# Mixture of experts in rounds of 3, 2, 2 and 1 with 64-row token tiles, wider weight rows, and six raw with three split weight buffers

## The chip, the core and the metric

The kernel runs on one core of a Trainium2 chip. The metric is device time in microseconds (us), the median of repeated executions. One execution is also profiled; its trace gives each engine's instructions, the transfers and the waits. The engines are TensorE (PE in the rows, PEld for its loads of stationary operands), VectorE (DVE), ScalarE (ACT), GpSimd (POOL) and SyncE (SP), whose queue issues the weight transfers.

## The reference, cut to what matters

A model of four blocks works on 256 tokens of 1024 features in float32. The part that the change touches is the mixture of experts at the end of the second block:

```python
def moe_ffn(x, router_w, w1, w3, w2):
    logits = (xt @ router_w).astype(F32)
    top_v, top_i = lax.top_k(logits, TOP_K)            # TOP_K = 2 of 8
    ...
    for e in range(N_EXPERTS):
        y = y + gates[:, e:e + 1].astype(x.dtype) * swiglu(xt, w1[e], w3[e], w2[e])
```

`swiglu(x, w1, w3, w2)` is `(silu(x @ w1) * (x @ w3)) @ w2`, with `w1` and `w3` of 1024 x 3584 and `w2` of 3584 x 1024 for each expert, 44 MB an expert. The inputs are fixed. The reference's router puts 134, 122, 80, 51, 48, 37, 28 and 12 tokens on its eight experts, in order of size; every other stage of the model works on all 256 tokens.

## The kernel before, in words

**Units.** All weights come as units of up to 1 MiB: `unit` (L168) has SyncE load 128 x 2048 floats into a raw buffer (tag `raw`), and `split` (L164) makes two float32r parts of it, `wh` on ScalarE (L165) and the rest `wl` on VectorE (L166). TensorE multiplies with both. Raw buffers come from pool `pw`, pairs `wh`/`wl` from pool `ph` (four of each before). SyncE may load a unit when VectorE has read the raw buffer's last content; the split may write when TensorE is done with the pair's last content.

**Slots.** `route` (L801) sorts the experts by their tokens: slot 0 has the most. The counts choose one of two plans, `few` or `many`, by a branch on a register. The inputs take `few`:

```python
few = [([(0, 0, False), (0, self.cap, True), (7, 0, True), (6, 0, True)],
        [[(0, (0, 1), None), (7, (2,), 0), (6, (3,), 1)]])]
few += [([(1, 0, False)], [one(1)])]
few += [([(s, 0, False), (s + 1, 0, False)], [one(s), one(s + 1, 1)]) for s in (2, 4)]
```

So the first round works on three experts in turn: slot 0 with a full tile of 128 tokens and a half tile of 64, and slots 7 and 6 with a half tile each. Slots 1 to 5 then have a full tile each, one expert after the other.

**Phases.** The hidden 3584 columns are cut in seven pieces `f` of 512. For one expert and one `f`, `up` (L952) takes two units each of `w1` and `w3` (four k-tiles of 128 rows, 512 columns), `turn` (L986) transposes the product (`uT`), and `down` (L1005) takes two units of `w2` (two k-tiles, 1024 columns): six units in all. A full tile needs three products for each k-tile and 512 columns (`wh` and `wl` with the high part of the tokens, `wh` with the low part), a half tile two, since its high and low parts lie side by side in one stationary operand of 128 columns and `wl` meets only the 64 high ones. In the trace a full tile shows as `ul`, a half tile as `uhl`. `phases` (L1149) alternates the experts of a round and puts `down` of a phase behind `up` of the next one. `finish` weighs the outputs and puts them back on their tokens. Slots 7 and 6 add their outputs up in SBUF (`ysum`), all other tiles in PSUM banks.

**Order.** `stream` (L1063) emits a unit's load and split two units ahead of the products. Each engine works through a list of its own that the compiler puts in order from this; engines wait on semaphores. The pools' sizes are one input of that order, so lists outside the mixture of experts change a little as well.

Of the kernel before, what the change touches and what calls it, by code (L numbers as in the profile page):

```python
# [11 lines left out]
F32R = mybir.dt.float32r  # L12
# [63 lines left out]
class Acc:  # L76
    """a PSUM region that n matmuls accumulate in; fresh: the first one clears the bank"""
# [30 lines left out]
class Gated:  # L108
    """a generator that comes to a halt ahead of job n until ready()"""
# [16 lines left out]
def blend(a, b, every):  # L126
    """a, with a step of b emitted after each `every` us of it"""
# [10 lines left out]
class Model:  # L138
# [145 lines left out]
    def run_a(self, src, c0, n, parts, x, nk=8, layout=None):  # L284
        """feature-layout product; parts: (bank, rows, column offset in bank, column offset in the unit)"""
# [19 lines left out]
    def feat(self, src, c0, nf, x, out):  # L305
        """nf tiles of 128 features, two to a bank: [128, f%2, tok]"""
# [3 lines left out]
    def to_feat(self, src, t, xh, xl):  # L310
        """src [128 tok, 1024] -> xh/xl[:, k, t*128:...] split transposed"""
# [20 lines left out]
    def bcast_row(self, dst, src):  # L332
        """DRAM vector [n] to all partitions of dst [128, n]"""
# [3 lines left out]
    def warm(self, func, after):  # L337
        """has the scalar engine's table for func loaded ahead of its use, once after [128, n] is there"""
# [6 lines left out]
    def rsqrt(self, v, eps):  # L345
        """v = (v + eps) ** -0.5 for a few columns, without a table of the scalar engine"""
# [1544 lines left out]
```

## Time and profile before

| | |
|---|---|
| median of 3 runs | 2378.1 us (2375.16 to 2379.86) |
| profiled execution, first to last instruction | 2376.3 us |
| mean granted TensorE clock | 0.989 of 2.4 GHz |
| first round of experts | about 447 to 855 us |
| rounds of slots 1 to 5 | about 855 to 1472 us |
| TensorE, VectorE, ScalarE busy | 96%, 74%, 59% of the span |

Busy times are sums over the span, so an engine with 74% can still be the limit of one stage. The stages are told apart by the windows in the section on rows. The trace gives no other time of the profiled execution than its span.

### The profile page before, as it was taken

How to read it: one execution, taken by the hardware profiler on the slowest of the kernel's cores; microseconds unless marked ns; L12 is line 12 of the kernel's file. 1: busy time of each engine (PE TensorE's matmuls, PEld its weight loads, DVE VectorE, ACT ScalarE, POOL GpSimd, SP SyncE). 2: the span in 40 equal slices, each digit the busy share in tenths (PEclk: the TensorE clock that was granted, in tenths of full speed). 3: DMA queues.
4: the chain of work that ended last, by engine and by line, in shares of the span. 5: the costliest groups of instructions: out<-in, count | busy, mean ns of one | idle time of the engine just before them, and what ended most of it. 6: DMA issues, size and time to landing. Idle time of an engine off the chain costs nothing. (4 is left out here: it accounts for less than half of the span.)

```text
span 2376.3 us, 29764 instructions
## 1 busy us (share of the span) xinstructions
PE 2285.2 (96%) x11444; PEld 1854.5 (78%) x11444; DVE 1770.3 (74%) x1907; ACT 1410.7 (59%) x1532; POOL 109.3 (5%) x154
## 2 busy tenths in 40 slices
PE   7999999799999989999999998899999999999998
PEld 6788886577777768887888776787888888888887
DVE  4665465798888998889888887898566459966653
ACT  5554354577777767677777775547554344764542
POOL 2100010100000000000000000100100001010000
PEclk9999999899999999999999999899999999999999
DMA  9456560699999989999999998553655554555552
GB/s 289 171 194 181 177 206 22 230 337 342 343 341 315 322 317 350 348 361 353 375 336 368 358 347 302 190 179 116 213 183 182 195 184 131 183 168 199 181 187 75
DMA packets 266967, 585.10 MB, mean 246 GB/s; under 512 B 10513, under 2 KB 21189, under 8 KB 266560
## 3 DMA queue, kind: packets, MB, share of 16 engines
q1 hardware_dynamic: 260880, 565.48, 68.7%
q0 software_dynamic: 5936, 17.64, 2.4%
q8 instruction: 91, 1.49, 0.3%
q14 instruction: 60, 0.49, 0.1%
HBM read 580.43 MB, written 2.64 MB: 245 GB/s over the span
## 5 line engine op out<-in xcount | busy, mean ns | idle before, releaser
L166 DVE TENSOR_TENSOR wl<-raw,wh 128x2048 fp32r<-128x2048 f32 (+2 forms) x532 | 1200.9, 2269 | 391.6 <-ACT wh L165 389.4
L165 ACT ACTIVATE wh<-raw 128x2048 fp32r<-128x2048 f32 (+2 forms) x532 | 1003.5, 1895 | 515.4 <-PE lin L84 145.1
L945 PE MATMUL lin<-wh,ring 128*128 128x512 f32 x1680 | 556.1, 392 | 0.0
L945 PE MATMUL lin<-wl,ring 128*128 128x512 f32 (+1 forms) x1008 | 399.0, 396 | 9.4 <-DVE wl L166 9.3
L945 PEld LDWEIGHTS lin<-wh,ring 128*128 128x128 f32 x1680 | 315.4, 188 | 81.2
L945 PEld LDWEIGHTS lin<-wl,ring 128*128 128x128 f32 (+1 forms) x1008 | 171.3, 170 | 63.2 <-DVE wl L166 23.2
L84 PE MATMUL lin<-wh,hh 128*128 128x512 f32 x352 | 142.0, 404 | 0.0
L84 PE MATMUL lin<-wl,hh 128*128 128x512 f32 x352 | 138.4, 393 | 2.3 <-DVE wl L166 2.3
L84 PE MATMUL lin<-wh,hl 128*128 128x512 f32 x352 | 138.0, 393 | 0.1
L945 PE MATMUL y<-wl,uh 128*128 128x512 f32 x336 | 107.6, 401 | 3.8 <-DVE wl L166 3.8
L1427 DVE SCALAR_TENSOR_TENSOR ro<-conv,ro 128x256 f32<-128x256 f32 x240 | 105.5, 474 | 0.4
L945 PE MATMUL y<-wh,ul 128*128 128x512 f32 x336 | 104.3, 391 | 0.0
L945 PE MATMUL y<-wh,uh 128*128 128x512 f32 x336 | 104.1, 390 | 0.0
L84 PE MATMUL lin<-wh,h2h 128*128 128x512 f32 x256 | 101.1, 395 | 0.0
L84 PE MATMUL lin<-wl,h2h 128*128 128x512 f32 x256 | 99.9, 390 | 0.2
L84 PE MATMUL lin<-wh,h2l 128*128 128x512 f32 x256 | 99.3, 390 | 0.2
L84 PE MATMUL lin<-wh,xah 128*128 128x512 f32 (+1 forms) x240 | 87.7, 366 | 0.7 <-ACT xah L165 0.6
L84 PE MATMUL lin<-wh,xal 128*128 128x512 f32 (+1 forms) x240 | 86.7, 364 | 0.0
L84 PE MATMUL lin<-wl,xah 128*128 128x512 f32 (+1 forms) x240 | 86.6, 361 | 0.0
L84 PEld LDWEIGHTS lin<-wl,hh 128*128 128x128 f32 x352 | 66.8, 190 | 16.1 <-DVE wl L166 3.2
L84 PEld LDWEIGHTS lin<-wh,hh 128*128 128x128 f32 x352 | 66.8, 190 | 15.7 <-issue 1.3
L84 PEld LDWEIGHTS lin<-wh,hl 128*128 128x128 f32 x352 | 66.7, 189 | 14.7 <-DVE hl L166 0.4
(543 smaller groups left out, 3781.0 us busy)
## 6 DMA issues: line engine op xcount, KB each, us to landing
raw<-in_moe_w SPq DMA_DIRECT2D x336, 1024.0 KB, 6.8
raw<-in_w_in SPq DMA_DIRECT2D x70, 1024.0 KB, 5.2
raw<-in_w_ff SPq DMA_DIRECT2D x64, 1024.0 KB, 5.2
raw<-in_ffn_w SPq DMA_DIRECT2D x32, 1024.0 KB, 5.1
raw<-in_w_out SPq DMA_DIRECT2D x12, 1024.0 KB, 8.2
raw<-in_w_branch SPq DMA_DIRECT2D x8, 1024.0 KB, 5.9
raw<-in_w_out SPq DMA_DIRECT2D x8, 512.0 KB, 8.3
raw<-in_w_branch SPq DMA_DIRECT2D x8, 512.0 KB, 6.4
```

The costliest lines, as they stand in the source:

```text
L84: nc.tensor.matmul(o, lhsT=lhsT, rhs=rhs, start=(self.i == 0 and self.fresh), stop=(self.i == self.n - 1), skip_group_check=True)
L165: self.nc.scalar.activation(h, src, AF.Copy)
L166: self.nc.vector.tensor_sub(l, src, h.bitcast(F32))
L945: nc.tensor.matmul(a.ap[:rows], lhsT=lhsT, rhs=u[part][:, kk, cs], start=(a.i == 0), stop=(a.i == a.n - 1), skip_group_check=True)
L1427: nc.vector.scalar_tensor_tensor(acc[:, f], uT[:, f, k:k + 256], cw[:, f, k:k + 1], acc[:, f], op0=OP.mult, op1=OP.add)
```

## The change

- `route` also tells whether slot 3 has at most 64 tokens; a third plan, `light`, is run then. It keeps the first round, and pairs slot 1 (full tile) with slot 5 (half tile), slot 2 with slot 4, and takes slot 3 (half tile) alone. With the reference's counts slot 3 has 51 tokens.
- An expert has a new argument `wide`, true where each expert of a round has one tile: all rounds but the first. `up` and `down` then take two `f` at a time, and a unit of `w1` or `w3` is two k-tiles by 1024 columns. In the first round the order is by pairs of `f` too: each expert does two pieces before the next one's turn.
- `w2` has a new layout `pairs` in all rounds: a partition holds two neighbouring rows, 8 KB in one piece; `turn` takes every second column of the product to match.
- The pools have six raw buffers and three split pairs in place of four and four.
- The first write of `ysum` goes from VectorE to ScalarE. Comments are taken out.

```diff
-        self.pw = ctx.enter_context(tc.tile_pool(name="pw", bufs=4))
-        self.ph = ctx.enter_context(tc.tile_pool(name="ph", bufs=4))
+        self.pw = ctx.enter_context(tc.tile_pool(name="pw", bufs=6))
+        self.ph = ctx.enter_context(tc.tile_pool(name="ph", bufs=3))
...
+        elif layout == "pairs":
+            nc.sync.dma_start(rv, src[ks[0] * 128:(ks[0] + nk) * 128, c0:c0 + n].rearrange("(p k) n -> p k n", k=nk))
...
+        nc.vector.tensor_scalar(fit[:, 3:4], cs[:, 3:4], 64.5, fit[:, 2:3], op0=OP.is_lt, op1=OP.mult)
+        nc.vector.tensor_add(fit[:, 4:5], fit[:, 2:3], fit[:, 3:4])
...
-        def up(f):
+        def up(f, nf):
             accs = {}
+            kn = 4 // nf
...
+                ks = list(range(kn * q, kn * q + kn))
...
-                            accs[name, i] = Acc(self.bank("lin"), 8 * per[i])
-                        products(z, z["x"], ks, u, [(accs[name, i], slice(0, 512))])
-                return (wt, ks, f * 512, 512), work
+                            accs[name, i] = [Acc(self.bank("lin"), 8 * per[i]) for _ in range(nf)]
+                        products(z, z["x"], ks, u, [(accs[name, i][c], cols(c)) for c in range(nf)])
+                return (wt, ks, f * 512, 512 * nf), work
...
+                    part = lambda j: s[:, 256 * (j // 2) + j % 2:256 * (j // 2) + 256:2]
...
-                return (w2, [4 * f + 2 * q, 4 * f + 2 * q + 1], 0, 1024), work
+                k = 4 * (f + c) + 2 * q
+                return (w2, [k, k + 1], 0, 1024, "pairs"), work
...
+        steps = [[(f, 2)] if wide else [(f, 1), (f + 1, 1)] for f in (0, 2, 4)] + [[(6, 1)]]
...
-                for f in range(7):
+                for i in range(4):
                     for e in es:
-                        jobs = e[0](f)
...
+                        for p in e[5][i]:
+                            jobs = e[0](*p)
...
+        first = ([(0, 0, False), (0, self.cap, True), (7, 0, True), (6, 0, True)],
+                 [[(0, (0, 1), None), (7, (2,), 0), (6, (3,), 1)]])
+        light = [first]
+        light += [([(s, 0, False), (h, 0, True)], [[(s, (0,), None), (h, (1,), None)]]) for s, h in ((1, 5), (2, 4))]
+        light += [([(3, 0, True)], [one(3)])]
...
+        with tc.If(n > 1) as cmp:
+            run(light)
```

Two places show how the lists move. The first is VectorE's list in the first round, in the middle of it, ahead of a `ul`; `wl` is the split of a unit, `sa<-lin,sa` the first step of a half tile, `sa<-sa,lin` the product of the two branches, `ul` and `uhl` the split of a transposed full or half tile. Before:

```order
L166 TENSOR_TENSOR uhl<-uT,uhl 128x4x64
L166 TENSOR_TENSOR wl<-raw,wh 128x2048 x3
L971 TENSOR_TENSOR sa<-lin,sa 64x512
L166 TENSOR_TENSOR wl<-raw,wh 128x2048
L980 TENSOR_TENSOR sa<-sa,lin 128x512
L166 TENSOR_TENSOR wl<-raw,wh 128x2048
L980 TENSOR_TENSOR sa<-sa,lin 128x512
L166 TENSOR_TENSOR wl<-raw,wh 128x2048
L1024 TENSOR_TENSOR ysum<-ysum,y 128x512 x2
L166 TENSOR_TENSOR wl<-raw,wh 128x2048
L166 TENSOR_TENSOR ul<-uT,uh 128x512
```

And now, from the piece between two `ul` that lies in slots 7 and 6:

```order
L166 TENSOR_TENSOR uhl<-uT,uhl 128x4x64
L166 TENSOR_TENSOR wl<-raw,wh 128x2048
L982 TENSOR_TENSOR sa<-lin,sa 64x512
L166 TENSOR_TENSOR wl<-raw,wh 128x2048 x2
L992 TENSOR_TENSOR sa<-sa,lin 128x512
L166 TENSOR_TENSOR wl<-raw,wh 128x2048 x2
L1038 TENSOR_TENSOR ysum<-ysum,y 128x512 x2
L166 TENSOR_TENSOR uhl<-uT,uhl 128x4x64
L166 TENSOR_TENSOR wl<-raw,wh 128x2048 x2
L982 TENSOR_TENSOR sa<-lin,sa 64x512
L166 TENSOR_TENSOR wl<-raw,wh 128x2048 x2
L992 TENSOR_TENSOR sa<-sa,lin 128x512
```

Before, 18 `wl` stood between one `ul` and the next, the six units of each of the three experts. Now two `ul` follow each other after 7 `wl`, and then 29 `wl` pass before the next `ul`: the two half-tile experts have their four pieces in one stretch.

The second place is VectorE's list in a later round, in the middle of its pieces. Before, with one expert at a time:

```order
L166 TENSOR_TENSOR wl<-raw,wh 128x2048 x4
L980 TENSOR_TENSOR sa<-sa,lin 128x512
L166 TENSOR_TENSOR wl<-raw,wh 128x2048 x2
L166 TENSOR_TENSOR ul<-uT,uh 128x512
```

And now, a full-tile expert (`ul`) and a half-tile expert (`uhl`) in turn:

```order
L166 TENSOR_TENSOR wl<-raw,wh 128x2048 x9
L992 TENSOR_TENSOR sa<-sa,lin 128x512 x2
L166 TENSOR_TENSOR wl<-raw,wh 128x2048 x2
L166 TENSOR_TENSOR ul<-uT,uh 128x512
L166 TENSOR_TENSOR wl<-raw,wh 128x2048
L166 TENSOR_TENSOR ul<-uT,uh 128x512
L166 TENSOR_TENSOR wl<-raw,wh 128x2048 x5
L982 TENSOR_TENSOR sa<-lin,sa 64x512 x2
L166 TENSOR_TENSOR wl<-raw,wh 128x2048 x4
L992 TENSOR_TENSOR sa<-sa,lin 128x512 x2
L166 TENSOR_TENSOR wl<-raw,wh 128x2048 x2
L166 TENSOR_TENSOR uhl<-uT,uhl 128x4x64
```

The number of `wl` for an expert and an `f` is six before and now. What stands around them has doubled in size and comes half as often.

## Rows read from the trace of the kernel before

**Rows 1.** The page's first line: the span.

```profile
span 2376.3 us, 29764 instructions
```

**Rows 2.** Windows (us): engines' busy time, granted clock, DMA share, GB/s.

```profile
core 0: us, PE busy (x) PEld busy (x) DVE busy (x) ACT busy (x) POOL busy (x), PEclk, DMA share, GB/s
447.00:855.00 408.00, 393.58 (x1803) 292.19 (x1802) 361.06 (x279) 304.34 (x255) 0.00 (x0) 1.00 0.94 330
855.00:1472.00 617.00, 608.09 (x2746) 493.25 (x2745) 540.53 (x348) 438.40 (x308) 0.00 (x0) 1.00 0.97 351
0.00:447.00 447.00, 407.44 (x2267) 340.86 (x2268) 257.94 (x418) 210.67 (x300) 43.21 (x71) 0.97 0.53 174
1500.00:2376.30 876.30, 864.91 (x4601) 720.42 (x4599) 588.27 (x831) 443.18 (x650) 60.12 (x71) 1.00 0.52 171
```

**Rows 3.** Groups by line and shape, 447 to 1472 us: busy us, mean ns, idle before.

```profile
L166 DVE TENSOR_TENSOR wl<-raw,wh 128x2048 fp32r<-128x2048 f32 x335 | 761.3, 2288 | 95.7 <-ACT wh L165 93.7
L165 ACT ACTIVATE wh<-raw 128x2048 fp32r<-128x2048 f32 x335 | 638.5, 1917 | 175.5 <-DMA raw<-in_moe_w 139.0 <-PE lin L945 25.1 <-PE y L945 3.7
L980 DVE TENSOR_TENSOR sa<-sa,lin 128x512 f32<-128x512 f32 x63 | 42.9, 683 | 19.2 <-PE lin L945 18.8
L166 DVE TENSOR_TENSOR ul<-uT,uh 128x512 fp32r<-128x512 f32 x42 | 28.7, 683 | 2.6 <-ACT uh L165 2.6
L971 DVE TENSOR_TENSOR sa<-lin,sa 64x512 f32<-64x512 f32 x21 | 14.3, 682 | 0.7
L166 DVE TENSOR_TENSOR uhl<-uT,uhl 128x256 fp32r<-128x256 f32 x21 | 8.7, 417 | 0.1
L1024 DVE TENSOR_TENSOR ysum<-ysum,y 128x512 f32<-128x512 f32 x24 | 15.3, 680 | 0.0
```

**Rows 4.** Timeline of TensorE, a later round: start us, us, engine, line, out<-in.

```profile
1024.22 0.39 PE L945 MATMUL lin<-wh,ring 128*128 128x512 f32 x1
...
1038.27 0.60 PE L999 MATMUL uT<-ident,sa 128*128 128x128 f32 x4
...
1041.11 0.39 PE L945 MATMUL lin<-wh,ring 128*128 128x512 f32 x1
```

**Rows 5.** The same of the first round.

```profile
544.89 0.39 PE L945 MATMUL lin<-wh,ring 128*128 128x512 f32 x1
545.12 0.40 PE L945 MATMUL lin<-wl,ring 128*64 128x512 f32 x1
...
548.14 0.69 PE L945 MATMUL y<-wl,uhl 128*64 128x512 f32 x2 [0.78 <-DVE wl L166]
...
630.80 0.60 PE L999 MATMUL uT<-ident,sa 128*128 128x128 f32 x4
631.24 1.00 PE L992 MATMUL uT<-route,sa 128*128 128x64 f32 x8
632.09 0.47 PE L945 MATMUL lin<-wh,ring 128*128 128x512 f32 x1
```

**Rows 6.** Windows: two f of the first round, then shorter and longer stretches.

```profile
497.64:608.17 110.53, 107.50 (x491) 79.45 (x490) 97.63 (x67) 83.70 (x66) 0.00 (x0) 1.00 0.96 339
1250.00:1300.00 50.00, 49.67 (x224) 40.65 (x224) 43.22 (x24) 36.84 (x24) 0.00 (x0) 1.00 1.01 373
0.00:50.00 50.00, 36.28 (x209) 30.67 (x210) 25.62 (x50) 26.94 (x28) 10.39 (x19) 1.00 0.90 275
428.00:440.00 12.00, 3.24 (x11) 2.94 (x12) 7.83 (x49) 0.63 (x3) 0.00 (x0) 0.50 0.13 30
```

**Rows 7.** Transfers of 1004 to 1009, then of 1009.2 to 1014.2 us.

```profile
DMA packets 974, 1.96 MB, mean 392 GB/s; under 512 B 21, under 2 KB 21, under 8 KB 974
...
DMA packets 500, 1.94 MB, mean 388 GB/s; under 512 B 23, under 2 KB 23, under 8 KB 499
```

**Rows 8.** Waits of 447 to 1472 us: us in total, times, longest.

```profile
ACT wh L165 <- DMA raw<-in_moe_w: 139.0, 143, 4.5
```

**Rows 9.** Timeline of VectorE: two splits in one row.

```profile
1010.02 4.49 DVE L166 TENSOR_TENSOR wl<-raw,wh 128x2048 fp32r<-128x2048 f32 x2 [0.74 <-ACT wh L165]
```

More of the change, by code (lines that the diff above doesn't have):

```diff
@@ L924, in gather, with expert @@
                         nc.vector.tensor_copy(d[1][:, k0:k0 + per], pv[:, :, c0:c0 + n])
-    def expert(self, tiles, w, acc):
+    def expert(self, tiles, w, acc, wide):
         nc = self.nc
@@ new lines, in gate @@
+                    for c in range(nf):
+                        p = accs["a", i][c].ap
+                        s = self.mid("sa")
+                        st[i]["s"].append(s)
+                        if z["half"]:
+                            nc.scalar.activation(s[64:128], p[64:128], AF.Copy)
+                            nc.vector.tensor_tensor(s[0:64], p[0:64], s[64:128], op=OP.add)
+                            nc.scalar.activation(s[64:128], s[0:64], AF.Silu)
+                            nc.scalar.activation(s[0:64], s[0:64], AF.Silu)
+                        else:
+                            nc.scalar.activation(s, p, AF.Silu)
@@ L986, in turn @@
-        def turn(f):
-            for i, z in enumerate(tiles):
-                s = st[i]["s"]
-                p = self.bank("uT")
-                if z["half"]:
-                    for j in range(4):
-                        nc.tensor.matmul(p[:, j * 64:(j + 1) * 64], lhsT=s[:, j * 128:(j + 1) * 128], rhs=self.twice,
-                                         start=True, stop=True)
-                    hl = self.mid("uhl", (128, 4, 128), dt=F32R)
-                    self.split(hl[:, :, 0:64], hl[:, :, 64:128], p[:, 0:256].rearrange("p (j c) -> p j c", c=64))
-                    st[i][f] = hl
-                else:
-                    for j in range(4):
-                        nc.tensor.transpose(p[:, j * 128:(j + 1) * 128], s[:, j * 128:(j + 1) * 128], self.ident)
-                    h, l = self.mid("uh", (128, 4, 128), dt=F32R), self.mid("ul", (128, 4, 128), dt=F32R)
-                    pv = p.rearrange("p (j c) -> p j c", c=128)
-                    self.split(h, l, pv)
-                    st[i][f] = (h, l)
@@ L1005, in down, with turn @@
-        def down(f):
-            def job(q):
+            n = 2 * nf
+            return [(*job(name, wt, q), then if q == n - 1 else none)
+                    for name, wt, then in (("a", w1, gate), ("b", w3, mul)) for q in range(n)]
+        def turn(f, nf):
+            for c in range(nf):
+                for i, z in enumerate(tiles):
+                    s = st[i]["s"][c]
+                    p = self.bank("uT")
+                    part = lambda j: s[:, 256 * (j // 2) + j % 2:256 * (j // 2) + 256:2]
+                    if z["half"]:
+                        for j in range(4):
+                            nc.tensor.matmul(p[:, j * 64:(j + 1) * 64], lhsT=part(j), rhs=self.twice, start=True, stop=True)
+                        hl = self.mid("uhl", (128, 4, 128), dt=F32R)
+                        self.split(hl[:, :, 0:64], hl[:, :, 64:128], p[:, 0:256].rearrange("p (j c) -> p j c", c=64))
+                        st[i][f + c] = hl
+                    else:
+                        for j in range(4):
+                            nc.tensor.transpose(p[:, j * 128:(j + 1) * 128], part(j), self.ident)
+                        h, l = self.mid("uh", (128, 4, 128), dt=F32R), self.mid("ul", (128, 4, 128), dt=F32R)
+                        pv = p.rearrange("p (j c) -> p j c", c=128)
+                        self.split(h, l, pv)
+                        st[i][f + c] = (h, l)
@@ L1007, in work, with down, job @@
+        def down(f, nf):
+            def job(c, q):
                 def work(u):
@@ L1009, in work @@
                         inner = z.get("sum") is not None
-                        if q == 0 and (f == 0 or inner):
-                            st[i]["y"] = [Acc(self.bank("y"), (4 if inner else 28) * per[i]) for c in range(2)]
-                        products(z, st[i][f], (2 * q, 2 * q + 1), u,
-                                 [(st[i]["y"][c], slice(c * 512, (c + 1) * 512)) for c in range(2)])
-                return (w2, [4 * f + 2 * q, 4 * f + 2 * q + 1], 0, 1024), work
+                        if c == q == 0 and (f == 0 or inner):
+                            st[i]["y"] = [Acc(self.bank("y"), (4 * nf if inner else 28) * per[i]) for _ in range(2)]
+                        products(z, st[i][f + c], (2 * q, 2 * q + 1), u, [(st[i]["y"][o], cols(o)) for o in range(2)])
+                k = 4 * (f + c) + 2 * q
+                return (w2, [k, k + 1], 0, 1024, "pairs"), work
             def add():
@@ L1019, in add, with then @@
                         for c in range(2):
-                            o, p = z["sum"][:, c * 512:(c + 1) * 512], st[i]["y"][c].ap
+                            o, p = z["sum"][:, cols(c)], st[i]["y"][c].ap
                             if f == 0:
-                                nc.vector.tensor_copy(o, p)
+                                nc.scalar.activation(o, p, AF.Copy)
                             else:
                                 nc.vector.tensor_add(o, o, p)
-            return [(*job(0), put_back if f == 6 else lambda: None), (*job(1), add)]
+            def then(c, q):
+                if c == q == 0 and f == 6:
+                    return put_back
+                return add if (c, q) == (nf - 1, 1) else lambda: None
+            return [(*job(c, q), then(c, q)) for c in range(nf) for q in range(2)]
         def put_back():
@@ L1059, in settle @@
             self.warm(AF.Sqrt, z[:, 0] if tiles[0]["half"] else z[0][:, 0])
-        return up, down, turn, finish, settle
+        steps = [[(f, 2)] if wide else [(f, 1), (f + 1, 1)] for f in (0, 2, 4)] + [[(6, 1)]]
+        return up, down, turn, finish, settle, steps
     def stream(self, jobs, ahead=2):
@@ L1203, in make @@
                                     zs[0]["sum"] = ysum[:, inner]
-                                es.append(self.expert(zs, weights(s), acc))
+                                es.append(self.expert(zs, weights(s), acc, all(len(x[1]) == 1 for x in r)))
                             return es
@@ L1220, in moe @@
         index[0] = nc.values_load(idi[0:1, 0:1], engines=[mybir.EngineType.SP], min_val=0, max_val=7)
[L1221 to L1223 removed]
+        n = nc.values_load(idi[0:1, 16:17], min_val=0, max_val=2)
+        with tc.If(n > 1) as cmp:
+            run(light)
         with cmp.Else():
[L1225 removed]
+            with tc.If(n > 0) as inner:
+                run(few)
+            with inner.Else():
+                run(many)
         self.xn = self.big("xn").rearrange("p (t d) -> p t d", d=D)
```

66 lines of the change are left out of this document (27 added, 39 removed).

## The prediction

> **What bounds the kernel now.** The page's first line comes first: a span of 2376.3 us [rows 1]. The windows by stage then tell which engine is full where [rows 2]. In the rounds of slots 1 to 5 (855 to 1472 us, 617 us) TensorE is busy for 608 us, VectorE for 541, and the transfers' share is 0.97 at 351 GB/s: TensorE sets the pace, but the transfers are right behind it. The first round (408 us) has TensorE at 394, VectorE at 361 and a share of 0.94. The two stretches outside move half as much (174 and 171 GB/s), and there TensorE leads VectorE by far: 407 against 258, 865 against 588. The groups of the experts' stretch [rows 3] give durations: a `wl` 2288 ns in the mean (two back to back 4.49 us, so 2.245 each, when nothing disturbs [rows 9]), a `wh` 1917 ns, a step of a tile 680 to 683 ns, `uhl` 417 ns. VectorE idles 95.7 us ahead of `wl`, nearly all of it for ScalarE's `wh`, and ScalarE idles 139 us for the raw data (143 times, longest 4.5 us [rows 8]). So a unit's way is transfer, `wh`, `wl`, TensorE, and any of four can be late.
>
> **TensorE's work for one f.** A full tile: from one `lin` on `ring` to the same point one piece later is 1041.11 - 1024.22 = 16.89 us [rows 4]. Matmuls follow each other after 0.23 us (544.89 to 545.12 [rows 5]). A half tile needs 48 of them instead of 72, six units of 8: 11.0 us, and about 0.85 for its turn (631.24 to 632.09 [rows 5]): 11.9 us. So a half tile saves 5.0 us of TensorE. It saves no bytes and no `wl`.
>
> **Later rounds.** Before, 35 expert-pieces of 16.89 us are 591 us, and 26 us go to gathering, finishing and round changes. Now slots 3, 4 and 5 are half tiles (21 pieces), slots 1 and 2 full ones (14). The floor of each engine:
> - TensorE: 14 x 16.89 + 21 x 11.9 + 26 = 512 us.
> - VectorE: a half tile has an `sa<-lin,sa` (0.682) more and a `uhl` (0.417) for a `ul` (0.683), +0.416 us a piece; 541 + 21 x 0.416 = 549 us.
> - Transfers: 210 units of 1.0486 MB are 220.2 MB. Five-microsecond stretches moved 392 GB/s with 2 KB packets (974 packets) and 388 with 4 KB ones (500 packets) [rows 7]: 220.2 MB at 390 is 565 us. Over 50 us TensorE's pace drew 373 at a share of 1.01 [rows 6]: 590 us. The stage as a whole had 351 at 0.97, that is 362 at a full share [rows 2]: 608 us.
>
> So TensorE gives way to the transfers, with VectorE close behind. The gain is 617 minus something between 565 and 608, 9 to 52 us. I take the middle, 586 us (376 GB/s, VectorE at 549/586 = 94%): **-31 us**. I don't go to the low end, since 390 was held for 5 us only, and since VectorE's 549 us would then have to fit at 97% behind a stream that it waits for.
>
> **Long rows.** 2 KB and 4 KB packets moved the same [rows 7], so the wide units are worth 0 here. 8 KB packets stand in no row; that they are slower nothing suggests, and at best they take the transfers to the low end above, so their bound is inside the range already. In the first round w2 alone changes, and TensorE with VectorE hides it.
>
> **Six raw buffers** let transfers run ahead of a late `wl`. They can take away some of ScalarE's 139 us of waits [rows 8], which are worth something only where transfers bound: inside the 9 to 52 again.
>
> **Eight banks.** A wide round of two experts holds four PSUM banks of outputs, two of `a` and two of `b`, all eight. A bank of `a` is free again after the `silu`, one of `b` after the product, and four units of other work lie between either and its next use, 7 us even in a half tile (4 x 8 x 0.23) against 2 x 0.683 us for two products and two `wl` ahead of them (4.5). Cost 0. If a `wl` more stands ahead, 2.2 us are lost at each of the 12 double phases: 27 us at worst, which would need VectorE late every time, and I leave that to the rival on VectorE.
>
> **First round.** TensorE needs 216 matmuls a piece, 216 x 0.23 = 49.7 us, and turns of about 3.0 us (0.6 to 1.0 each with what follows [rows 5]): 52.7, 105.4 for two. Two pieces took 110.53 us [rows 6], so 5.1 us a pair are waits, such as the 0.78 for a `wl` at 548.14 [rows 5]. Heavy units (slot 0, 20 matmuls, 4.6 us) let VectorE get ahead, light ones (8 matmuls, 1.84 us, less than a `wl`) use the lead up. Before, light stretches were 6 units long. By the new order they are 18: four of `up` and two of a neighbour's `down`, three times. There TensorE needs 18 x 1.84 + 3 x 0.85 = 35.7 us; VectorE 18 x 2.245 + 3 x (0.682 + 0.683 + 0.417 + 2 x 0.68) = 49.8 us, the last term being `ysum`. Three split buffers let VectorE be two units ahead, 4.5 us. The rest, 49.8 - 35.7 - 4.5 = 9.6 us, TensorE waits. If the 5.1 us of waits before are of this kind and go into it, the pair grows by 4.5 us, if they stay, by 9.6. I take 5, since the wait seen is of this kind; there are three pairs: **+15 us**. The ends are 0 (VectorE overtakes in the heavy units, or `ysum` is counted once less) and +29.
>
> **Three split buffers outside the experts.** There TensorE leads, with units of 12 matmuls or more. Only where light work changes to heavy could one buffer less show: at five such changes, each at most a `wh` and a `wl`, 1.92 + 2.29 = 4.2 us: 0 to 21. I take **+4**, one change, since no row shows how far VectorE is ahead there and TensorE leads it so widely [rows 2].
>
> **Small things.** Two tiny operations in `route` are some 0.3 us. `ysum`'s first copy on ScalarE has room (304 of 408 us busy [rows 2]). Every second column as a stationary operand stands in no row: I take 0, since loads run beside matmuls (PEld 493 us under 608 [rows 2]); if each turn took twice its 0.6 to 1.0 us [rows 5], the later rounds would hide it under the transfers, and the 28 turns of the first round would cost about 22 us.
>
> **Sum.** 2376.3 - 31 + 15 + 4 = 2364.3 us of span. The median lies 1.8 above the span of the profiled execution: **2366 us**, 0.5% faster.
>
> **Rivals.**
> *VectorE makes the first round slower than that.* In two pieces before it was busy 97.63 of 110.53 us, 88% [rows 6]. If it does no better in the light stretch, 49.8 becomes 56.6 us and TensorE waits 16.4 us a pair, 11 to 16 more than before; at 14 it is +42 us. Then 2378.1 - 31 + 42 + 4 = 2393, slower. It decides from 9 us a pair on, 27 in all. For it speaks that `wl` meets all other work on one queue, against it that two `wl` follow each other without a gap where raw data are there [rows 9].
> *The transfers are at their ceiling.* If the full-share rate of 362 GB/s holds, the later rounds take 608 us: -9 + 15 + 4, 2388 us, slower. For it speaks that the share is 0.97 already; against it 392 and 373 [rows 6, 7]. The Trainium skill, "HBM Reference", § Specifications (TRN2), gives about 358 GB/s as a core's share, by which the estimate for these 220.2 MB would be 615 us and the gain nil; the same section says that a core alone measures well above it. The trace disagrees with the lower figure: 373 over 50 us.
> *Both go well.* The first round no slower, nothing lost outside, transfers at 390: -52, 2326 us. For it speaks that deeper raw buffers take away what the transfers wait for.
> *The clock falls.* In the last round TensorE is busy 11.9 us of some 16.7, 71%. From 428 to 440 us, at 27%, the granted clock was 0.50 (1.2 of 2.4 GHz); at 73%, from 0 to 50 us, it was 1.00 [rows 6], so I hold it unlikely. At 0.46 us a matmul a piece takes 23.6 us, 7 x 6.9 = 48 more: 2414 us.
> *The plan isn't taken:* out, as slot 3 has 51 tokens.
>
> **Chances.** Forecast 0.58 (own range 2345 to 2386), VectorE 0.12, ceiling 0.12, both well 0.15, clock 0.03. The range reaches to the price of the VectorE rival above and near to that of the good case below: 2331 to 2393 us. A measurement tells about 0.2% here, 4.8 us, so 2373.3 to 2382.9 is no change. Of the forecast 0.45 lie faster, 0.11 within and 0.02 slower; of the rivals 0.15 faster, 0.03 within (ceilings a little above 362), 0.24 slower: 0.60, 0.14, 0.26.
>
> **What would show it.** The later rounds last 586 us at some 376 GB/s, with TensorE busy about 490 and waiting for `wl`, behind raw data. The first round lasts some 423 us in place of 408, its waits for `wl` lying in one stretch of slots 7 and 6 for each two pieces, whose period is 115.5 us. Ahead of 447 us and behind the experts nothing moves by more than 4. Packets of 8 KB move as fast as the others. I am wrong if the later rounds stay above 605 (ceiling), go below 570, or if the first round takes over 435.

## The result, and the profile after

The changed kernel takes 2408.2 us in the median (2406.71 to 2410.16, 4 runs) against 2378.3 for the kernel before: a ratio of 1.0132, 95% interval 1.0117 to 1.0146. It is slower by about 30 us, or 1.3%; 2366 was forecast, with a range up to 2393.

Three marks of TensorE cut the execution: the first `lin` of an expert, the first `sct` (slot 0 puts its outputs back, with some pieces of slots 7 and 6 still to come, alike in all kernels) and the last group of eight `sct`. Groups of `sct` in the trace of before (shortest, median and longest in ns, then first and last start in us):

```profile
L84 PE MATMUL sct<-y,gt x72: 387/389/502, 823.2 to 1475.1; 128*128 128x512 f32 x72
L84 PE MATMUL sct<-y,gt x8: 389/396/502, 1473.1 to 1475.1; 128*128 128x512 f32 x8
```

The same of after, then its first `lin`, from the timeline:

```profile
L84 PE MATMUL sct<-y,gt x72: 387/393/504, 855.1 to 1497.0; 128*128 128x512 f32 x72
L84 PE MATMUL sct<-y,gt x8: 387/397/504, 1495.0 to 1497.0; 128*128 128x512 f32 x8
```

```profile
448.64 0.39 PE L950 MATMUL lin<-wh,ring 128*128 128x512 f32 x1
```

With 447.37 for the first `lin` of before and the two spans (2376.3 [rows 1] and 2404.9) this gives:

| us | first `lin` to first `sct` ("first") | to the last group ("later") | outside (before and behind) |
|---|---|---|---|
| before | 375.9 | 649.9 | 1350.6 |
| after | 406.5 | 639.9 | 1358.6 |
| difference | **+30.6** | **-10.0** | **+8.0** |
| forecast, by the term | +15 | -31 | +4 |

These marks shift the limit between the two stages against [rows 2], but they cover the same work in all kernels, so the differences can be compared with the terms. They come from one profiled execution of each kernel. Executions of the kernel before lay between 2370 and 2384 us in all, so 2 or 3 us between two stages say nothing.

Windows of after (as in [rows 2]: busy us of PE, PEld, DVE, ACT, POOL, granted clock, DMA share, GB/s): two pieces of the first round, the later stretch, four pieces of a double round, two pieces of slot 3 alone:

```profile
583.70:704.90 121.20, 110.86 (x490) 80.09 (x489) 97.94 (x67) 83.09 (x66) 0.00 (x0) 0.99 0.87 312
855.10:1495.00 639.90, 570.28 (x2448) 409.40 (x2446) 572.97 (x405) 476.73 (x368) 0.00 (x0) 0.97 0.94 348
1213.50:1281.00 67.50, 61.90 (x265) 45.32 (x264) 59.35 (x35) 51.29 (x36) 0.00 (x0) 0.97 0.98 371
1425.80:1458.50 32.70, 26.81 (x114) 16.36 (x113) 29.79 (x19) 26.40 (x20) 0.00 (x0) 1.00 0.99 380
```

Two pieces of the first round take 121.2 us where they took 110.53 [rows 6]. Four pieces of the double rounds take 67.5: that is 16.9 a piece, just what a full tile took before [rows 4], though half of the pieces now need 5 us less of TensorE. No compute engine is full there: VectorE has 59.35 of 67.5 us, TensorE 61.90 with short waits and a slower clock in it. The transfers have a share of 0.98 at 371 GB/s, the rate that TensorE drew before [rows 6].

What is late there shows in the waits of the later stretch (us in total, times, longest; a loader's queue, ScalarE, TensorE):

```profile
SPq L191 <- DVE wl L166: 290.9, 121, 9.7
SPq L184 <- DVE wl L166: 160.0, 65, 7.9
ACT wh L165 <- PE lin L950: 51.1, 59, 4.7
ACT sa L981 <- PE lin L950: 34.0, 11, 4.2
PE lin L950 <- DVE wl L166: 44.8, 38, 3.2
```

SyncE waits 451 us for a raw buffer that VectorE has not read yet, and no wait of ScalarE for raw data is left among the large ones (before 139 us [rows 8], of which 120 in the later stretch). ScalarE waits for TensorE to free a pair and for its sums; TensorE waits for VectorE. VectorE's own list, in the same pieces (the idle time before an instruction stands in brackets), and then a step of ScalarE:

```profile
1203.22 4.50 DVE L166 TENSOR_TENSOR wl<-raw,wh 128x2048 fp32r<-128x2048 f32 x2 [1.18 <-PE lin L950]
1207.91 2.29 DVE L166 TENSOR_TENSOR wl<-raw,wh 128x2048 fp32r<-128x2048 f32 x1 [0.20 <-ACT wh L165]
1211.17 1.28 DVE L992 TENSOR_TENSOR sa<-sa,lin 128x512 f32<-128x512 f32 x2 [0.96 <-PE lin L950]
...
1220.18 11.09 DVE L166 TENSOR_TENSOR wl<-raw,wh 128x2048 fp32r<-128x2048 f32 x5
1231.30 1.28 DVE L982 TENSOR_TENSOR sa<-lin,sa 64x512 f32<-64x512 f32 x2
1233.58 2.29 DVE L166 TENSOR_TENSOR wl<-raw,wh 128x2048 fp32r<-128x2048 f32 x1 [1.00 <-ACT wh L165]
1237.73 6.70 DVE L166 TENSOR_TENSOR wl<-raw,wh 128x2048 fp32r<-128x2048 f32 x3 [1.85 <-ACT wh L165]
```

```profile
1230.53 1.08 ACT L981 ACTIVATE sa<-lin 64x512 f32<-64x512 f32 x2 [2.72 <-PE lin L950]
```

In the heavy part VectorE waits for TensorE, to free a pair (1203) and for its sums (1211). In the light one it runs without a gap (11.09 us) and then waits for ScalarE, which itself waited for the half tile's sums (2.72 us). Each engine is late in turn. What of this is cause had to be tried.

### The profile page after: what moved, and what is told of

Its sections match the earlier page's. It is cut to its first block, busy times and chain, and to the rows that moved or that the text cites. A ratio compares the mean times of both kernels' runs of the same rounds, so it can differ in the third digit from the quotient of the medians.

```text
span 2404.9 us, 29054 instructions
## 1 busy us (share of the span) xinstructions
PE 2227.5 (93%) x11024; PEld 1750.4 (73%) x11024; DVE 1772.3 (74%) x1936; ACT 1429.1 (59%) x1578; POOL 97.4 (4%) x154
## 5 line engine op out<-in xcount | busy, mean ns | idle before, releaser
L950 PE MATMUL lin<-wh,ring 128*128 128x512 f32 x1344 | 447.5, 401 | 11.6 <-DVE ysum L1038 5.9
L950 PE MATMUL lin<-wl,ring 128*64 128x512 f32 (+1 forms) x1008 | 371.1, 408 | 56.4 <-DVE wl L166 51.3
L950 PEld LDWEIGHTS lin<-wh,ring 128*128 128x128 f32 x1344 | 257.3, 192 | 94.4 <-ACT wh L165 11.2
L950 PEld LDWEIGHTS lin<-wl,ring 128*64 128x64 f32 (+1 forms) x1008 | 152.8, 157 | 140.6 <-DVE wl L166 98.5
L950 PE MATMUL y<-wl,uhl 128*64 128x512 f32 x336 | 107.7, 402 | 22.7 <-DVE wl L166 20.1
L950 PE MATMUL y<-wh,uhl 128*128 128x512 f32 x336 | 104.6, 393 | 3.1 <-ACT wh L165 3.1
L950 PEld LDWEIGHTS y<-wl,uhl 128*64 128x64 f32 x336 | 41.0, 134 | 57.3 <-DVE wl L166 41.8
L950 PEld LDWEIGHTS y<-wh,uhl 128*128 128x128 f32 x336 | 62.5, 188 | 25.8 <-ACT wh L165 4.7
```

What stands on the lines that cost most here:

```text
L950: nc.tensor.matmul(a.ap[:rows], lhsT=lhsT, rhs=u[part][:, kk, cs], start=(a.i == 0), stop=(a.i == a.n - 1), skip_group_check=True)
```

## The experiments

All stage lengths are by the three marks, from one trace of each run. The ratio is to the kernel before on the same chip. e5, e6 and e9 leave out parts of the weights, as their texts say, and are no kernels to use.

| run | time, us | ratio (95%) | first | later | outside |
|---|---|---|---|---|---|
| e1_pools44 | 2413.2 | 1.0157 (1.0137 to 1.0176) | 399.1 | 663.8 | 1348.5 |
| e2_before63 | 2399.0 | 1.0095 (1.0078 to 1.0112) | 399.2 | 639.4 | 1358.8 |
| e3_forder | 2401.7 | 1.0115 (1.0098 to 1.0132) | 397.7 | 640.6 | 1360.8 |
| e4_lightonly | 2398.1 | 1.0097 (1.0081 to 1.0114) | 376.5 | 662.8 | 1351.6 |
| e5_halfwl | 2382.9 | 1.0029 (1.0012 to 1.0046) | 397.5 | 620.7 | 1361.9 |
| e6_halfdma | 2385.0 | 1.0037 (1.0022 to 1.0053) | 406.8 | 616.6 | 1364.0 |
| e7_ahead3 | 2379.3 | 1.0018 (1.0000 to 1.0036) | 377.1 | 649.4 | 1350.7 |
| e8_before543 | 2394.3 | 1.0069 (1.0048 to 1.0091) | 382.6 | 636.8 | 1375.5 |
| e9_bothhalf | 2296.8 | 0.9667 (0.9641 to 0.9694) | 374.2 | 560.6 | 1361.3 |
| e10_singles | 2399.0 | 1.0097 (1.0075 to 1.0120) | 406.6 | 630.6 | 1359.4 |
| e11_fifthraw | 2365.0 | 0.9953 (0.9934 to 0.9971) | 374.5 | 638.7 | 1349.5 |
| e12_fifthhalf | 2378.4 | 1.0009 (0.9996 to 1.0022) | 375.5 | 654.3 | 1349.2 |
| e13_singles_fifth | 2360.8 | 0.9932 (0.9913 to 0.9950) | 377.7 | 630.2 | 1351.4 |
| e14_lategate | 2380.7 | 1.0017 (1.0005 to 1.0030) | 374.2 | 653.7 | 1348.4 |

**The parts taken apart.** The pools alone:

```diff
-        self.pw = ctx.enter_context(tc.tile_pool(name="pw", bufs=6))
-        self.ph = ctx.enter_context(tc.tile_pool(name="ph", bufs=3))
+        self.pw = ctx.enter_context(tc.tile_pool(name="pw", bufs=4))
+        self.ph = ctx.enter_context(tc.tile_pool(name="ph", bufs=4))
```

> The changed kernel with the pools of before: four raw buffers and four split pairs. It measures 2408 us now; its first round takes 406 us to the first put-back product (before 376), its later rounds 640 (before 650), the rest 908 (before 901). Theory of the split buffers: in heavy stretches VectorE and ScalarE wait for TensorE to free a pair, in light ones TensorE waits for VectorE, and one pair more gives one unit more of lead at each change. Then the first round falls to 390 to 396 us, the later rounds to 600 to 615, the rest to 901 to 903: 2350 to 2375 us. Rival, transfers at their ceiling near 350 GB/s: later rounds stay at 635 to 650, and with four raw buffers not better: 2395 to 2415. Rival, the order by two pieces alone: the first round stays above 400 and the rest gains 7, 2395 to 2402.

The reverse edit in the kernel before (six and three in place of four and four):

> The kernel before with six raw buffers and three split pairs, nothing else changed. Theory of the split buffers: where TensorE leads evenly (later rounds of before) one pair less costs little, 650 to 655 us; the first round with its short light stretches some 5 to 15 us more; the rest 5 to 8 us more, as in the changed kernel: 2386 to 2402 us. Rival, the pools cost only outside the experts: 2383 to 2386. Rival, deeper raw buffers help and one split pair less is nothing: 2365 to 2378, with the 7 us of the rest then due to something else.

The order in the first round:

```diff
-                    for e in es:
-                        for p in e[5][i]:
+                    for j in range(len(es[0][5][i])):
+                        for e in es:
+                            p = e[5][i][j]
```

> The changed kernel with the first round's experts changing after every piece of 512 columns, as before, in place of every two; later rounds and pools as changed. Theory of the order by two pieces: the first round goes back from 406 to 376 to 385 us, all else stays, 2378 to 2387 us. Theory of the split buffers: with three pairs the first round gets back only part, 385 to 395, 2388 to 2398. Rival, the 8 KB rows of w2 or the strided stationary operand slow the first round: it stays above 400, 2403 to 2410.

And the plan alone: the two edits above, `False` for `wide`, the old layout of `w2` and `part = lambda j: s[:, j * 128:(j + 1) * 128]`:

> The light plan alone: the kernel before with four raw and four split buffers, one piece of 512 columns at a time everywhere, short rows for w1, w3 and w2, the transposes of neighbouring columns, and only the new rounds and half tiles (and the first ysum copy on ScalarE). Theory of the split buffers: heavy and light pieces alternate after six units, the stretches are half as long and VectorE is three units ahead, so the later rounds take 590 to 605 us with the first round and the rest as before: 2330 to 2350. Rival, transfers at their ceiling: later rounds 635 to 650, 2365 to 2380. Rival, the half tiles themselves cost VectorE and ScalarE what they save on TensorE: 620 to 635, 2350 to 2365.

These four and the two kernels fill a square for the first round. With four and four and a change of expert after each piece it takes 375.9 (before) and 376.5 (e4); six and three alone make it 399.2 and 397.7 (e2, e3), two pieces at a time alone 399.1 (e1), both 406.5. So either alone costs 22 to 23 us, both 31. That the two don't add up fits a lead of VectorE that each uses up, but this is a reading: in e2 VectorE's list has another order as well, so buffers and order are not taken apart. The rows of `w2` and the strided operand add nothing (e2 against e3), nor do the new plan and the first write of `ysum` on ScalarE (before against e4). The 8 us outside go with the pools in all of them, 1348 to 1352 with four and four, 1359 to 1361 with six and three.

The later stretch of e1 and e4 fell out against every theory. Six and three alone bring the whole -10 (e2, with full tiles). The first rounds of e1 and e3 lie a little above what their theories of the split buffers had (390 to 396 and 385 to 395 us). The time of e2 lies within the range of its theory only since two misses cancel: the first round lost 23 us where 5 to 15 were expected, and the later rounds gained 10 where they were to lose up to 5. The new rounds and half tiles bring nothing with six and three (639.4 against 639.9 and 640.6) and cost 13 us with four and four (649.9 against 662.8 and 663.8), where e1 was expected at 600 to 615; why they cost that with four raw buffers was not taken apart. Long rows and two pieces a step show no effect there (e1 against e4).

**What binds the later stretch.** Half of VectorE's splitting (the experts get a unit of their own, and a line of `products` changes):

```diff
+    def unit_half(self, src, ks, c0, n, layout=None):
...
+        nc.scalar.activation(h, raw, AF.Copy)
+        nc.vector.tensor_sub(l[:, :1024], raw[:, :1024], h[:, :1024].bitcast(F32))
...
-                        nc.tensor.matmul(a.ap[:rows], lhsT=lhsT, rhs=u[part][:, kk, cs], start=(a.i == 0),
+                        nc.tensor.matmul(a.ap[:rows], lhsT=lhsT, rhs=u[part][:, kk % (len(ks) // 2) if part else kk, cs], start=(a.i == 0),
```

> The changed kernel, where VectorE forms `wl` of the experts' units for the first half of the columns only and TensorE uses that half twice; transfers, ScalarE's split and the matmuls are as many as before (it leaves out the low part of half of the weights). Some 1.1 us less of VectorE for each of 336 units. Theory that VectorE with the waits around it is the bound of the later rounds: they fall from 640 us to 565 to 600, where transfers or TensorE take over, and the first round from 406 to 375 to 385: 2310 to 2345 us. Rival, transfers at their ceiling: the later rounds stay at 630 to 645, and only the first round falls: 2370 to 2395. Rival, ScalarE waits in its list for TensorE, whatever VectorE does: 610 to 630.

Half of the bytes, again by a unit of its own, `twice` being the loaded half read two times:

```diff
+    def unit_short(self, src, ks, c0, n, layout=None):
...
+            nc.sync.dma_start(rv[:, :nk // 2], rows.rearrange("(p k) n -> p k n", k=nk)[:, :nk // 2])
...
+        twice = raw[:, :1024].rearrange("p (o n) -> p o n", o=1).to_broadcast([128, 2, 1024])
+        self.split(h.rearrange("p (o n) -> p o n", o=2), l.rearrange("p (o n) -> p o n", o=2), twice)
```

> The changed kernel, where only half of each of the experts' units is loaded (512 KB) and the split reads that half twice; the work of ScalarE, VectorE and TensorE is as before (it leaves out half of the weights). Theory that VectorE and the waits around it bind: nothing changes, later rounds 630 to 645, first round 400 to 410, 2398 to 2412 us. Theory of transfers at their ceiling: the later rounds fall to 580 to 600, 2345 to 2370. In between, if transfers slow VectorE by sharing memory: `wl` falls from 2.27 to 2.20 us and the later rounds by 10 to 20, 2385 to 2395.

And both edits at once:

> The changed kernel with both halves at once: half of each of the experts' units is loaded and split, and `wl` is formed for half of its columns (it leaves out half of the weights and of their low part). Half of VectorE's work alone brought the later rounds from 640 to 621 us, half of the transfers alone to 617; four pieces (24 units, full and half tile) then took 65.7 and 64.4 us in place of 67.5. Theory of two limits side by side (transfers at about 16.1 us a piece, VectorE at 15.1 busy and some waits): with both gone TensorE's 57.6 us or ScalarE's some 53 with its waits are left, 58 to 61 us, and the later rounds take 575 to 595, 2340 to 2362 in all. Rival, what binds is that ScalarE's and VectorE's lists wait in order for TensorE with three pairs: 63 to 65 us stay, later rounds 605 to 617, 2370 to 2388.

The windows of the later stretch, one row of each of these three kernels:

```profile
847.90:1468.60 620.70, 563.69 (x2447) 404.15 (x2445) 355.26 (x404) 470.04 (x368) 0.00 (x0) 0.98 0.96 359
```

```profile
860.90:1477.50 616.60, 556.65 (x2448) 406.81 (x2446) 572.27 (x405) 478.14 (x368) 0.00 (x0) 0.98 0.61 183
```

```profile
825.00:1385.70 560.70, 538.21 (x2448) 408.71 (x2446) 353.75 (x405) 473.14 (x368) 0.00 (x0) 0.99 0.66 201
```

With VectorE down from 573 to 355 us the stretch is 19 us shorter, with half of the bytes 23, with both 79. Neither was "the" bound: with VectorE relieved the transfers have a share of 0.96 (359 GB/s), with the transfers relieved VectorE is busy for 572 of 616.6 us (93%), and the one keeps what the other gives free. Only with both gone does TensorE set the pace again (538 of 560.7, 96%). Of the texts, e5's last rival (ScalarE waits in its list for TensorE, 610 to 630) had the 620.7 us. But its steps are as many in e9, and there the stretch is 560.7 us, far below the 605 to 617 of e9's own rival by the lists and below the 575 to 595 of its theory. Transfers that slow VectorE are out as well: with half of the bytes a `wl` took 2286 ns in the mean, with all of them 2287.

**Leads in the lists.** Two edits of the kernel before, `ahead=3` for `ahead=2` in `stream`, and pools of five `raw`, four `wh` and three `wl`:

> The kernel before (four and four buffers) with units emitted three ahead of their products in place of two; the lists of ScalarE and VectorE then hold one split more ahead of each step that waits for TensorE. Theory that the lists' order, not the pool's size, sets the lead: first round 376 to 365 to 372, later rounds 650 to 635 to 645, 2350 to 2370 us. Rival, the raw buffers bind with four (ScalarE's 120 us of waits for data in the later rounds): no change there, 2370 to 2380. Rival, steps that wait longer behind splits delay TensorE (product, turn): 2380 to 2400.

> The kernel before with five raw buffers, four `wh` and three `wl`, the same memory as four, four and four. Six raw and three pairs gave the later rounds 639 in place of 650, cost the first round 23 and the rest 8 us. If the loss came from `wh`, which ScalarE writes first and holds longest, then the first round stays at 376 to 382, the rest at 1351 and the later rounds fall to 640 to 646: 2362 to 2376 us. If it came from `wl`, all stays as with six and three, 2390 to 2400.

e7 told nothing about a longer lead, since the lists did not get one. Between two `ul` of a later round VectorE still has four `wl`, the product and two `wl`, as before, and in the middle of the first round the lists of VectorE and ScalarE have the order of before:

```profile
1061.63 4.56 DVE L166 TENSOR_TENSOR wl<-raw,wh 128x2048 fp32r<-128x2048 f32 x2 [0.17 <-ACT wh L165]
1068.15 2.29 DVE L166 TENSOR_TENSOR wl<-raw,wh 128x2048 fp32r<-128x2048 f32 x1 [1.96 <-ACT wh L165]
1070.68 2.29 DVE L166 TENSOR_TENSOR wl<-raw,wh 128x2048 fp32r<-128x2048 f32 x1 [0.24 <-ACT wh L165]
1073.33 0.69 DVE L980 TENSOR_TENSOR sa<-sa,lin 128x512 f32<-128x512 f32 x1 [0.36 <-PE lin L945]
1073.93 4.49 DVE L166 TENSOR_TENSOR wl<-raw,wh 128x2048 fp32r<-128x2048 f32 x2
1078.34 0.68 DVE L166 TENSOR_TENSOR ul<-uT,uh 128x512 fp32r<-128x512 f32 x1
```

Three `wl` (e8) cost the first round 7 and the outside 25 us, more than six and three did there. Neither of its two theories had these stages, though the time lies in the range of the second; why the outside suffers so was not followed up. The later stretch takes 636.8 us with full tiles and five raw buffers: it seems to be the raw buffers that help it, and the next run keeps four pairs to tell.

**Versions that use this.** Memory for a fifth raw buffer beside four pairs is there once the first round is over, in `ysum`:

```diff
-        raw = self.pw.tile([128, 2048], F32, tag="raw", name="raw")
+        raw = fifth if fifth is not None else self.pw.tile([128, 2048], F32, tag="raw", name="raw")
...
+                    self.taken += 1
+                    units.append(self.unit(*j[0], fifth=self.fifth if self.taken > 140 and self.taken % 5 == 0 else None))
...
+        self.fifth = self.big("ysum")
```

> The kernel before (four raw, four pairs), where the buffer of `ysum`, idle after the first round, serves as a fifth raw buffer for every fifth unit of the later rounds. Theory that the later rounds of before wait for raw data since four raw buffers are too few (120 us of ScalarE's waits; 639 and 637 us in place of 650 with six and five raw buffers): later rounds 636 to 642, first round 374 to 378 and the rest 1349 to 1353 as before, 2362 to 2372 us. Rival, it was the fewer pairs that helped there: 648 to 651, 2374 to 2380.

That came as its theory said: 638.7 later, nothing lost elsewhere, 0.9953 of the time before. The lists have the order of before, and the pairs are four, so the raw buffers alone do it. ScalarE's waits for data in the later stretch, before and in e11, with TensorE at 630 of 638.7 us in e11:

```profile
ACT wh L165 <- DMA raw<-in_moe_w: 120.4, 121, 4.5
ACT wh L165 <- DMA raw<-in_moe_w: 28.4, 27, 2.9
```

Half tiles one expert at a time, in the changed kernel (`[one(s), one(h, 1)]` in `light` for the pair) and in the version above (`[([(s, 0, s > 3), (s + 1, 0, True)], ...) for s in (2, 4)]` in `few`):

> The changed kernel with the same half tiles, wide units and pools, but slots 1, 5, 2, 4 and 3 one after the other in place of full and half in turn. Theory of two limits: a half tile alone goes at 16.0 to 16.4 us a piece (as slot 3 does in the last round), a full one at 16.9, in turn 16.9 in the mean, so 14 pieces of slots 4 and 5 gain 7 to 13 us: later rounds 625 to 635, 2391 to 2400 in all. Rival, the turn of full and half evens out what each lacks: 645 to 660, 2412 to 2427.

> As the run with the fifth raw buffer, and slots 3, 4 and 5 as half tiles, one expert after the other (a plan for these inputs: it takes their fit in 64 rows as given). Theory of two limits: a half tile's piece takes 16.0 to 16.4 us in place of 16.9, 21 pieces, 10 to 18 us less: later rounds 620 to 630, 2348 to 2360 us. Rival, with five raw buffers half tiles go at 17 to 18 us, as the 18 of the light plan with four: later rounds 640 to 660, 2366 to 2388.

The first gained 9 us, as expected. The second was 16 us slower than with full tiles: a half tile's piece took 17.4 us and more, where a full one takes 16.8. ScalarE's list in such pieces, then VectorE's:

```profile
1413.52 0.39 ACT L165 ACTIVATE uhl<-uT 128x256 fp32r<-128x256 f32 x1 [1.69 <-PE uT L992]
1420.00 0.59 ACT L970 ACTIVATE sa<-lin 64x512 f32<-64x512 f32 x1 [2.49 <-PE lin L945]
1430.96 0.39 ACT L165 ACTIVATE uhl<-uT 128x256 fp32r<-128x256 f32 x1 [1.71 <-PE uT L992]
1437.43 0.59 ACT L970 ACTIVATE sa<-lin 64x512 f32<-64x512 f32 x1 [2.48 <-PE lin L945]
```

```profile
1422.57 2.29 DVE L166 TENSOR_TENSOR wl<-ysum,wh 128x2048 fp32r<-128x2048 f32 x1 [1.26 <-ACT wh L165]
1425.68 2.29 DVE L166 TENSOR_TENSOR wl<-raw,wh 128x2048 fp32r<-128x2048 f32 x1 [0.82 <-ACT wh L165]
```

From one `uhl` to the next is 17.44 us. In it ScalarE stands 2.49 us for the sums of `w1` and 1.71 for the turned product, with splits behind them in its list, and VectorE then waits 2.08 us for `wh`. The last two runs tell whether that is a price of each step:

> The changed kernel with four raw buffers, four pairs and the buffer of `ysum` as a fifth raw buffer in the later rounds, the first round changing experts after each piece as before, and slots 1, 5, 2, 4, 3 one after the other, two pieces at a time with long rows. Theory of ScalarE's list, which waits in order for TensorE once a step: half tiles at 32 to 32.6 us for two pieces as with six and three (12.0 steps of two and single ones), first round 375 to 378, later rounds 622 to 634, rest 1349 to 1353: 2348 to 2365 us. Rival, six raw buffers are what lets half tiles go fast: 35 us for two pieces, later rounds 650 to 660, 2376 to 2390.

```diff
+            g = gate if n > 1 or not tiles[0]["half"] or tiles[0].get("sum") is not None else None
...
-            return [(*job("a", w1, 0, 0), none), (*job("a", w1, 1, 0), gate),
-                    (*job("b", w3, 0, 0), none), (*job("b", w3, 1, 0), mul)]
+            return [(*job("a", w1, 0, 0), none), (*job("a", w1, 1, 0), g or none),
+                    (*job("b", w3, 0, 0), none if g else gate), (*job("b", w3, 1, 0), mul)]
```

> The run with half tiles one by one and the fifth raw buffer, with one thing changed: in a half tile's piece the copy of the lower rows and what follows it (the gate) are emitted behind the first unit of `w3` in place of the last of `w1`, so one split more stands ahead of it on ScalarE and VectorE. Theory of ScalarE's list: the 46.6 us that it waits there for TensorE fall to under 20, a half tile's piece from 17.7 to 16.6 to 17.2 us, the later rounds from 654 to 630 to 645, 2355 to 2370. Rival, the number of raw buffers: 650 to 656, 2374 to 2382.

With two pieces a step and the same five and four buffers (e13) the turns of a half tile stand 32.6 us apart for two pieces, 16.3 a piece, and the stretch takes 630.2 us:

```profile
1265.19 1.98 PE L1007 MATMUL uT<-route,sa 128*128 128x64 f32 x16
1297.85 1.99 PE L1007 MATMUL uT<-route,sa 128*128 128x64 f32 x16
```

So six raw buffers are not needed for it. e13 is the fastest kernel here that leaves nothing out, 0.9932 of the time before; its interval overlaps that of e11. With four raw buffers two pieces a step had brought nothing (e1 against e4), so they don't do it by themselves. The later gate (e14) told nothing: the gate stands at the same place of ScalarE's list as in e12, with the same waits (46.9 us in place of 46.6), since the order was decided by other things than where it was emitted. That ScalarE's wait alone makes the difference is therefore argued, not shown; e13 differs from e12 in its rows of 4 and 8 KB and its order of slots too, and its later stretch was granted a clock of 0.99 in place of 0.97.

## Why the prediction was wrong, point by point

**Later rounds: the term was mis-sized (-31 forecast, -10 measured), and its cause was not the one named.** The failing step is the floor of the transfers. I set 565 to 608 us for all 210 units and compared it with a stage that had 26 us of round changes in it, which I had counted for TensorE alone. Piece by piece the room was small: a piece of before took 16.89 us at 373 GB/s; at the 371 and 380 GB/s of the windows of after, 6.29 MB take 16.6 to 17.0 us, and slot 3 alone took 16.35 (32.7 for two). So of TensorE's 5 us a half tile some half a us was to be had before the transfers and VectorE stood in the way. The -10 that came is due to the raw buffers alone: e2 has it with full tiles, and e11 with four pairs. I had put these "inside the 9 to 52 again" as a help to transfers that would bind; but it was before, with TensorE as the bound, that four raw buffers were too few.

**VectorE and the transfers as one bound.** I took the larger of two floors. e5, e6 and e9 show that two floors of nearly one height give more than either. The stretch took 640 us, where VectorE was busy for 573 and the 223 MB that were moved (348 GB/s over 639.9 us) need 586 to 600 at 380 to 371 GB/s; taking one away gave 19 and 23 us, both 79. That three pairs and lists that run in order are what joins the two is argued, not shown.

**First round: the waits came as forecast, but the sum left a second limit out (+15 forecast, +30.6 measured).** I had 4.5 to 9.6 us a pair and took 5; two pieces grew by 10.7. The waits of before did not go into the new one. They are of `wl`, as forecast, and a bank shows too (`PE lin`, 1.95 us for `ysum`, in a light stretch):

```profile
587.19 0.77 PE L950 MATMUL lin<-wh,ring 128*128 128x512 f32 x1 [1.95 <-DVE ysum L1038]
...
645.69 0.68 PE L950 MATMUL y<-wl,uhl 128*64 128x512 f32 x2 [1.29 <-DVE wl L166]
```

The failing step is that I counted VectorE alone in the light stretch and put the transfers at nothing there ("TensorE with VectorE hides it"). Its 18 units are 18.9 MB, some 53 us at the 357 to 359 GB/s that two windows of 40 us in such stretches moved: an estimate, and no less than the 49.8 that I had for VectorE. The windows below run from the second `ul` of a pair to the next `ul` (29 `wl`), in after, e5, e6 and e9; the last two are those of 40 us, of after and e5.

```profile
620.10:708.70 88.60, 78.26 (x348) 54.81 (x347) 79.01 (x55) 67.81 (x53) 0.00 (x0) 1.00 0.94 339
616.00:706.00 90.00, 82.56 (x356) 58.24 (x355) 49.47 (x56) 67.17 (x52) 0.00 (x0) 0.96 0.93 332
625.90:714.50 88.60, 78.33 (x349) 54.75 (x347) 79.03 (x55) 67.82 (x53) 0.00 (x0) 1.00 0.58 172
611.50:692.00 80.50, 77.86 (x356) 56.65 (x355) 49.49 (x56) 67.87 (x53) 0.00 (x0) 1.00 0.64 189
640.00:680.00 40.00, 32.55 (x140) 20.56 (x138) 39.51 (x26) 34.84 (x28) 0.00 (x0) 1.00 0.99 357
640.00:680.00 40.00, 33.78 (x135) 21.71 (x134) 22.46 (x25) 30.99 (x26) 0.00 (x0) 0.91 0.99 359
```

In the light stretch of after VectorE is full (39.51 of 40 us) and the transfers too (share 0.99). With half of VectorE's splitting the stretch is no shorter (90.0 against 88.6 us), at the same share of the transfers; with half of the bytes neither (88.6); with both it falls to 80.5, and the whole first round to 374.2. If VectorE had been the one limit, as in my sum, e5 should have taken the growth away; it took 9 of 31 us. (e5 was granted a clock of 0.96 over its 90.0 us, which can have cost at most 3.6 us, an estimate.) I charged the term to the order and the pools together, and overlooked that three pairs alone would cost the old order 23 us (e2).

**Outside: right in kind, +8 for +4,** and within 0 to 21; e1 to e4 tie it to the pools.

**What held.** The plan was taken. The turn with every second column costs what it did: eight transposes take 1.11 us, where four took 0.60 [rows 4].

```profile
1213.50 1.11 PE L1013 MATMUL uT<-ident,sa 128*128 128x128 f32 x8
```

The eight PSUM banks cost nothing that shows in the later stretch: no large wait of TensorE there is for a bank. The transfers' share by the Trainium skill, "HBM Reference", § Specifications (TRN2), about 358 GB/s a core, is not the limit here: 371 over 67.5 us and 380 over 32.7 stand above it in this trace.

**The rivals.** The VectorE rival had the first round at +42 and the sum at 2393; the ceiling rival had -9 for the later rounds and 2388. Both halves came about together, +30.6 and -10.0, and their sum lies above either: I had given each its own chance, and none to both. The first rival's point of decision, 27 us, was passed, but not for its reason: VectorE was not held to 88% in the light stretch, it was full there (39.51 of 40 us), and the transfers with it. That -10.0 lies so near to the ceiling rival's -9 is luck: the same -10 came with full tiles from the raw buffers (e2, e11). The clock rival was set in the last round, where 1.00 was granted (1425.8 to 1458.5); the clock fell in the double rounds instead, as the last section shows.

## What to carry to other kernels

- Before taking work off the engine that leads, work out per step what the next two or three resources need, round changes included. Where they lie within a few per cent, the saving is worth only that difference. Relieving one alone then shows little (19 and 23 us here), so an experiment must relieve two at once (79).
- Buffers between three engines can be read as a lead in time: here one pair less, and light stretches three times as long, cost the first round 23 us each and 31 together. Count a pool's change for every stage, not for the one that it is meant for.
- Memory that is idle in one stage can be the missing buffer of another (0.5% here, without a change of the work).

## What was unexpected in the hardware

TensorE's clock fell between matmuls that followed each other with short waits. In a light stretch of after, TensorE waited 0.68 and 1.59 us; the window of 1233.8 to 1240.5 us was granted 0.75 in the mean, and that of 1236 to 1238 us 0.50, the lower level of 1.2 GHz. Pairs of matmuls that took 0.62 us took 1.05 there, before they were back at 0.63:

```profile
1233.80:1240.50 6.70, 4.36 (x12) 2.48 (x12) 4.84 (x3) 6.68 (x7) 0.00 (x0) 0.75 0.99 393
1236.00:1238.00 2.00, 2.00 (x5) 1.32 (x6) 0.27 (x1) 2.00 (x2) 0.00 (x0) 0.50 1.01 410
```

```profile
1233.60 0.73 PE L950 MATMUL lin<-wh,ring 128*128 128x512 f32 x2 [0.68 <-ACT wh L165]
1235.93 1.11 PE L950 MATMUL lin<-wl,ring 128*64 128x512 f32 x2 [1.59 <-DVE wl L166]
1236.84 1.05 PE L950 MATMUL lin<-wh,ring 128*128 128x512 f32 x2
...
1240.58 0.63 PE L950 MATMUL lin<-wh,ring 128*128 128x512 f32 x2
```

I had this rival for the last round alone, at 48 us. It comes in short dips, and in this one some three pairs at 0.43 us more each are 1.3 us. Over the later stretch 0.97 was granted, where before had 1.00 [rows 2]: 0.03 of 639.9 us is 19 us, the most that the dips can have cost there (an estimate). Whether they lengthen the stretch, or only come with waits that do, no run here separates. Transfers with rows of 4 and 8 KB ran at 371 to 380 GB/s in the windows above, no faster than the 392 and 388 of [rows 7].
